# Keys and values of the dilated attention: projected in token order, then put into the group's order

## The chip, the cores and the metric

The kernel runs on one core of a Trainium2 chip. The metric is the device time of one execution in microseconds; the kernel before takes 1798.36 us (median of three runs, 1797.4 to 1800.12). One further execution was profiled, and every row below is from that one.

## What is computed

One transformer layer on 1024 tokens of width 1024, in float32. After a norm, the hidden states `h` are projected by one wide matrix. Its columns feed a gated linear attention and three groups of dilated attention (4 heads of 128). What matters here is a group's order of tokens:

```
DIL_PATTERNS = ((128, 1), (512, 4), (2048, 16))      # window, dilation
k = rms_norm(heads(k, 128), dil_k_norm_g[l, gi])     # q too; v without a norm
to_sub(t): t.reshape(B, S // dilation, dilation, H, E), the two token axes swapped, padded
           to blocks of 128: block b of residue d holds tokens d, d + dilation, ...
scores of a block of queries against its own and the previous block of keys, softmax, times v
```

Dilation 4 has four residues of 256 tokens, so two blocks each. Dilation 16 has sixteen of 64 tokens; the kernel puts two of them (d and d + 8) into one block of 128 and masks across them. Behind attention come the mix of the branches, the output projection, the router and the experts, which the change does not touch.

## The kernel before, in words

`h` is transposed and split into a high and a low part of fp32r (`hT`, tiles named strip, width first, tokens along the free dimension). Every weight quarter (128 x 1024, 512 KB) is loaded on SP's queue into `w_raw` (three buffers), and a cast on ScalarE (L131) and a subtraction on VectorE (L132) make its high and low part (`part`, five buffers). A matmul of the projections is three: high with high, high with low, low with high (`mm3`, L241 to L243).

A projection of one tile (`project`, L316) makes 128 tokens by 512 columns: eight steps over the width, three matmuls each, 24 in all. The stationary operand, which a weight load brings in before each matmul, is 128 tokens of `hT`; the moving one is 512 columns of weights. Which 128 tokens a tile holds is what `tokens` (L307) says: 128 neighbours for group 0 (dilation 1), every fourth of 512 for group 1 (dilation 4), every eighth of 1024 for group 2 (dilation 16). In the two wider groups the stationary operand is thus read with a step of four or eight elements, and the products come out in the group's order.

The groups go 2, 1, 0. `k_stage(g)` projects eight key tiles; `normed` (L336) squares a tile on ScalarE, sums on VectorE, takes the root on ScalarE, multiplies on VectorE, and one tile later four transposes on TensorE (L349, into one of two banks named tp) and a scaled copy on ScalarE (L350) put it into `kT` (tiles named ka, five buffers of two key tiles). `k_stage(2)` is woven into the last head's recurrence of the linear attention, four of its steps for one of the recurrence; `k_stage(1)` and `k_stage(0)` begin in the last three tiles of the attention before (L459) and finish alone.

`attention(g, ...)` projects eight value tiles, one after another without a transpose except the last key tile's behind value tile 0; each is copied out of its bank by ScalarE (L384) into tiles named kb. Then come queries 0, 1 and 2, each normalised and transposed like a key tile, scores (L403), softmax, transposes of the probabilities (L418) and the products with the values (L431), whose results go to DRAM (L435). The maxima and sums of the softmax go through DRAM into token order (L482 to L488) and are read back, much later in the program, by the combine stage (L687).

The program is written in one order. A scheduler then makes each engine's and each queue's order: it goes through time with its own costs, and an instruction whose inputs and buffers are ready is placed before one that is not, with program order deciding among those that are. Each engine and queue then works strictly in the order made. Dependencies on tiles, in DRAM too, become waits.

Of the kernel before, what the change touches and what calls it, by code (L numbers as in the profile page):

```python
# [9 lines left out]
F32 = mybir.dt.float32  # L10
# [5 lines left out]
AF = mybir.ActivationFunctionType  # L16
OP = mybir.AluOpType
# [3 lines left out]
S = 1024  # L21
# [3 lines left out]
NT = 8  # L25
# [119 lines left out]
def run(gen):  # L145

    while True:
        try:
            next(gen)
        except StopIteration as e:  # L150
            return e.value
# [20 lines left out]
def kernel_body(tc, out, x, w_in, w_alr, w_a2, gains, b_gate, w_mix, g1, g2, g2c, w_r, b_r, w_gate, w_up, w_down,  # L172
                c_mats, c_bias, c_slots):
    nc = tc.nc
    es = ExitStack()
    consts = es.enter_context(tc.tile_pool(name="consts", bufs=1))
    dram = es.enter_context(tc.tile_pool(name="dram", bufs=1, space=bass.MemoryType.DRAM))
# [12 lines left out]
    def acc():  # L190
        return ps_acc.tile([128, 512], F32, name="acc")

    def tp():
        return ps_tp.tile([128, 512], F32, name="tp")
# [6 lines left out]
    def t2k(shape=(128, 512), dt=F32):  # L201
        return work.tile(list(shape), dt, name="t2k", bufs=n2k)
# [4 lines left out]
    def ka4(shape=(128, 1024), dt=F32):  # L207
        return kv.tile(list(shape), dt, name="ka", bufs=5)

    def kb4(shape=(128, 1024), dt=F32):  # L210
        return kv.tile(list(shape), dt, name="kb", bufs=4)
# [3 lines left out]
    sr_dram = dram.tile([3, 64, 128], F32, name="sr_dram")  # L215
    st_dram = dram.tile([3, 8, S], F32, name="st_dram")
    f_dram = dram.tile([3, H, S], F32, name="f_dram")
    yg_dram = dram.tile([KT, 128, S], F32, name="yg_dram")
    zt_dram = dram.tile([NT, 128, KT, 128], F32, name="zt_dram")
    h2_dram = dram.tile([S, D], F32, name="h2_dram")  # L220
# [18 lines left out]
    def mm3(ps, a, b, first, last):  # L239
        (ah, al), (bh, bl) = a, b  # L240
        nc.tensor.matmul(ps, ah, bh, start=first, stop=False)  # L241
        nc.tensor.matmul(ps, ah, bl, start=False, stop=False)  # L242
        nc.tensor.matmul(ps, al, bh, start=False, stop=last)  # L243
# [14 lines left out]
    def rsqrt(rs, ss, n):  # L258
        nc.scalar.activation(rs, ss, AF.Ln, bias=eps, scale=1.0 / n)
        nc.scalar.activation(rs, rs, AF.Exp, scale=-0.5)  # L260
# [16 lines left out]
    for n in range(NT):  # L277
# [11 lines left out]
        for q in range(2):  # L289
            pt = tp()  # L290
# [9 lines left out]
    gcol = consts.tile([128, 7], F32, name="gcol")  # L300
# [6 lines left out]
    def tokens(ap, g, i):  # L307

        if g == 0:
            return ap[:, 128 * i:128 * i + 128]  # L310
        if g == 1:
            d, b = divmod(i, 2)
            return ap[:, 512 * b + d:512 * b + 512:4]
        return ap[:, i::8]

    def project(ps, g, i, units, act=None):  # L316

        act = act or hT
        for k in range(KT):
            hi, lo = units[k // 2]  # L320
            j = 512 * (k % 2)
            mm3(ps, (tokens(act[k][0], g, i), tokens(act[k][1], g, i)), (hi[:, j:j + 512], lo[:, j:j + 512]), k == 0, k == KT - 1)
            yield
# [12 lines left out]
    def normed(ps, gain, res):  # L336

        sq = t2k()
        nc.scalar.activation(sq, ps, AF.Square)  # L339
        ss = small.tile([128, 4], F32, name="ss4")  # L340
        nc.vector.tensor_reduce(ss, sq.rearrange("p (h e) -> p h e", h=4), axis=AX.X, op=OP.add)  # L341
        rs = small.tile([128, 4], F32, name="rs4")
        rsqrt(rs, ss, 128)
        nc.vector.tensor_tensor(sq.rearrange("p (h e) -> p h e", h=4), ps.rearrange("p (h e) -> p h e", h=4),
                                rs[:, :, None].to_broadcast([128, 4, 128]), op=OP.mult)
        yield
        pt = tp()
        for h in range(4):
            nc.tensor.transpose(pt[:, 128 * h:128 * h + 128], sq[:, 128 * h:128 * h + 128], ident)  # L349
        nc.scalar.activation(res, pt, AF.Copy, scale=gain)  # L350

    def k_stage(g):
        units = W.take(4)
        kT = []
        for i in range(NT):
            if i % 2 == 0:
                t = ka4()
            kT.append(t[:, 512 * (i % 2):512 * (i % 2) + 512])
        last = None
        for i in range(NT):  # L360
            ps = acc()
            yield from project(ps, g, i, units)
            if last is not None:
                run(last)
            last = normed(ps, gcol[:, 4 + g:5 + g], kT[i])
            next(last)
        return kT, last

    def attention(g, kT, last, after):
# [4 lines left out]
        units = W.take(4)  # L374
        v = []
        for i in range(NT):
            ps = acc()
            run(project(ps, g, i, units))
            if i == 0:
                run(last)  # L380
            if i % 2 == 0:
                t = kb4()
            v.append(t[:, 512 * (i % 2):512 * (i % 2) + 512])
            nc.scalar.copy(v[i], ps)  # L384
        units = W.take(4)

        def query(i):
            ps = acc()
            yield from project(ps, g, i, units)
            return ps  # L390
# [46 lines left out]
        def normq(ps):  # L437
            res = t2k()
            g_ = normed(ps, qg[:, g:g + 1], res)
            next(g_)  # L440
            return res, g_
# [12 lines left out]
        ps = run(query(2))  # L454
        run(qn[1][1])
        for i in range(NT):
# [12 lines left out]
            if i < NT - 3:  # L469
                ps = run(fill)  # L470
# [3 lines left out]
        pt = tp()  # L474
# [16 lines left out]
    units = W.take(4)  # L491
    v = []
    for b in range(NT):
        ps = acc()
        run(project(ps, 0, b, units))
        if b % 2 == 0:
            t = kb4()
# [14 lines left out]
    for hf in range(2):  # L512
        cols = slice(512 * hf, 512 * hf + 512)
        ps = acc()
# [48 lines left out]
    for j in range(2):  # L563
        t = kv.tile([128, 512], F32, name=f"att{j}", bufs=1)
# [78 lines left out]
    for h in range(H):  # L643
        _, qk = weave(recur(h, *qk), heads(h + 1) if h < H - 1 else k_stage(2), 2 if h < H - 1 else 4)

    units = {}

    def gr(j):

        if j % 2 == 0:  # L650
            units[j // 2] = W.take(1)[0]
        ps = acc()
        yield from columns(ps, cut(units[j // 2], 0, KT), j % 2)
        return ps
# [7 lines left out]
    for g in (2, 1, 0):  # L662
        after = k_stage(g - 1) if g > 0 else gr_start()
        attention(g, *qk, after)
        qk = run(after)
# [3 lines left out]
    for h in range(H):  # L669
        og = w4k()  # L670
        nc.sync.dma_start(og, og_dram[:, h])
        for hf in range(2):
            j = 2 * h + hf
            ps = qk[j] if j < 3 else run(gr(j))
            t = t2k()
# [28 lines left out]
    for c in range(KT):  # L704
# [3 lines left out]
        for hf in range(2):  # L708
            ps = acc()
# [79 lines left out]
    for e in range(NE):  # L789
        for w in (w_gate, w_up):  # L790
            v = w[e].rearrange("(p k) c -> p k c", k=KT)
            experts += [v[:, 2 * u:2 * u + 2] for u in range(4)]
        v = w_down[e].rearrange("(p k) c -> p k c", k=4)
# [304 lines left out]
    with tc.For_i(0, todo, 1) as i:  # L1098
        sp = (mybir.EngineType.SP,)
        e = nc.values_load(lst[0:1, bass.ds(i, 1)], engines=sp, min_val=0, max_val=NE - 1)  # L1100
        b = nc.values_load(lst[0:1, bass.ds(i + 16, 1)], engines=sp, min_val=0, max_val=6)
# [6 lines left out]
        v = w_down[bass.ds(e, 1)].rearrange("o (p k) c -> p (o k) c", k=4)  # L1108
# [26 lines left out]
```

## Time and profile before

| | |
|---|---|
| median of three runs | 1798.36 us |
| the profiled execution | 1798.59 us |
| its span (first to last instruction) | 1796.7 us |
| TensorE busy (matmuls) | 1763.9 us, 98% of the span |
| weight loads busy (beside matmuls) | 1493.9 us, 83% |
| VectorE, ScalarE, GpSimd busy | 59%, 50%, 6% |
| memory traffic | 324.44 MB, 181 GB/s in the mean |

PE is TensorE's matmuls, PEld its weight loads, which overlap the matmul before. A matmul's recorded duration is longer than its share of a stream, since matmuls are pipelined; the distance from start to start is what one costs. SPq is SP's queue, which issues nearly all transfers; its rows are issues and not transfers. Of the span, attention with its projections lies from about 200 to 760 us, the experts from about 1180 us on.

### The profile page before, as it was taken

The page shows a single profiled execution, that of the slowest core. Times are in us where ns is not written, and L with a number is a line of the kernel's source. Part 1 is how long each engine was busy: PE and PEld are TensorE (multiplying, and loading weights), DVE is VectorE, ACT ScalarE, POOL GpSimd, SP SyncE. Part 2 cuts the span into 40 slices and gives each one's busy share as a digit, 9 for nine tenths or more (in the row PEclk, how much of TensorE's full clock was granted, in tenths as well). Part 3 has the DMA queues.
Part 4 walks back from the last instruction along what each step waited for, and adds up shares of the span by engine and source line. Part 5 has one row for each costly group of instructions (what it writes and reads, how often), then busy time and mean ns, then how long its engine had stood idle before and what let it go on. Part 6 is the DMA issues. An engine that isn't in the chain of part 4 may idle for free.

```text
span 1796.7 us, 23091 instructions
## 1 busy us (share of the span) xinstructions
PE 1763.9 (98%) x8603; PEld 1493.9 (83%) x8603; DVE 1059.1 (59%) x1554; ACT 904.3 (50%) x1464; POOL 115.9 (6%) x110
## 2 busy tenths in 40 slices
PE   8999999999999999999999999999999999999996
PEld 7788899999998888887888878887777777777775
DVE  6375550442145225657232256769999899998985
ACT  6453341443244324433121143358787888888774
POOL 0000000000000000000000011121111111111110
PEclk9999999999999999999999999999999999999999
DMA  6111100122102110469331289579999999999992
GB/s 214 47 36 59 48 28 31 59 78 66 47 18 81 58 47 25 131 194 281 101 105 59 90 271 287 181 236 351 366 358 350 347 354 353 354 358 357 354 362 80
DMA packets 123217, 324.44 MB, mean 181 GB/s; under 512 B 25808, under 2 KB 42784, under 8 KB 123088
## 3 DMA queue, kind: packets, MB, share of 16 engines
q1 hardware_dynamic: 112512, 304.83, 48.2%
q0 software_dynamic: 10016, 17.78, 4.1%
q8 instruction: 68, 1.11, 0.3%
q10 hardware_dynamic: 576, 0.34, 0.1%
q14 instruction: 45, 0.37, 0.1%
HBM read 297.49 MB, written 42.43 MB: 189 GB/s over the span
## 4 chain that ended last, share of the span: by engine, by line
PE 75%; DMA 15%; DVE 5%; issue 2%; ACT 2%; SPq 0%; POOL 0%; DVEq 0%; POOLq 0%; ACTq 0%
PE acc L241 19%; PE acc L242 19%; PE acc L243 19%; DMA m_raw<-in_w_down_dram 3%; DMA m_raw<-in_w_up_dram 2%; DMA n_raw<-in_w_gate_dram 2%; DMA n_raw<-in_w_up_dram 2%; PE mm L241 2%; PE mm L243 2%; PE mm L242 2%; PE mm L403 2%; PE mm L431 2%; DVE part L132 1%; DVE m_part L132 1%; PE tp L349 1%
## 5 line engine op out<-in xcount | busy, mean ns | idle before, releaser
L132 DVE TENSOR_TENSOR part<-w_raw,part 128x1024 fp32r<-128x1024 f32 x111 | 135.5, 1221 | 256.3 <-ACT part L131 255.8
L241 PE MATMUL acc<-part,strip 128*128 128x512 f32 x640 | 276.0, 432 | 1.0 <-ACT part L131 1.0
L242 PE MATMUL acc<-part,strip 128*128 128x512 f32 x640 | 257.3, 402 | 1.5 <-DVE part L132 1.5
L243 PE MATMUL acc<-part,strip 128*128 128x512 f32 x640 | 256.6, 401 | 0.0
L132 DVE TENSOR_TENSOR part<-m_raw,part 128x1024 fp32r<-128x1024 f32 x173 | 209.4, 1221 | 26.7 <-ACT part L131 24.2
L131 ACT CAST part<-m_raw 128x1024 fp32r<-128x1024 f32 x173 | 180.5, 1055 | 45.6 <-PE acc L243 27.9
L241 PE MATMUL acc<-strip,part 128*128 128x512 f32 x448 | 181.7, 406 | 0.9 <-ACT t2k L747 0.9
L242 PEld LDWEIGHTS acc<-part,strip 128*128 128x128 f32 x640 | 172.6, 270 | 11.7 <-DVE part L132 2.3
L241 PEld LDWEIGHTS acc<-part,strip 128*128 128x128 f32 x640 | 170.3, 266 | 11.6 <-ACT part L131 1.7
L243 PEld LDWEIGHTS acc<-part,strip 128*128 128x128 f32 x640 | 170.6, 267 | 11.3 <-DVE strip L256 0.2
L243 PE MATMUL acc<-strip,part 128*128 128x512 f32 x448 | 176.2, 393 | 0.0
L242 PE MATMUL acc<-strip,part 128*128 128x512 f32 x448 | 175.5, 392 | 0.0
L131 ACT CAST part<-w_raw 128x1024 fp32r<-128x1024 f32 x111 | 116.6, 1051 | 108.7 <-PE acc L243 92.2
L132 DVE TENSOR_TENSOR m_part<-m_raw,m_part 128x1024 fp32r<-128x1024 f32 x104 | 126.5, 1218 | 5.4 <-ACT m_part L131 5.2
L241 PE MATMUL acc<-part,xT 128*128 128x512 f32 x320 | 128.1, 400 | 0.0
L243 PE MATMUL acc<-part,xT 128*128 128x512 f32 x320 | 126.8, 396 | 0.0
L242 PE MATMUL acc<-part,xT 128*128 128x512 f32 x320 | 125.9, 393 | 0.8 <-DVE part L132 0.8
L131 ACT CAST m_part<-m_raw 128x1024 fp32r<-128x1024 f32 x104 | 109.6, 1056 | 17.4 <-PE mm L243 8.7
L341 DVE TENSOR_REDUCE ss<-t2k 128x4 f32<-128x512 f32 x48 | 32.9, 685 | 133.6 <-ACT t2k L339 133.6
L241 PEld LDWEIGHTS acc<-strip,part 128*128 128x128 f32 x448 | 84.3, 188 | 18.9 <-ACT t2k L747 1.4
L243 PEld LDWEIGHTS acc<-strip,part 128*128 128x128 f32 x448 | 84.2, 188 | 18.7
L242 PEld LDWEIGHTS acc<-strip,part 128*128 128x128 f32 x448 | 84.3, 188 | 18.3 <-issue 1.2
(274 smaller groups left out, 3321.6 us busy)
## 6 DMA issues: line engine op xcount, KB each, us to landing
m_raw<-in_w_up_dram SPq DMA_DIRECT2D x96, 512.0 KB
m_raw<-in_w_gate_dram SPq DMA_DIRECT2D x91, 512.0 KB
m_raw<-in_w_down_dram SPq DMA_DIRECT2D x90, 512.0 KB
w_raw<-in_w_in_dram SPq DMA_DIRECT2D x52, 512.0 KB
w_raw<-in_w_mix_dram SPq DMA_DIRECT2D x32, 512.0 KB
n_raw<-in_w_down_dram SPq DMA_DIRECT2D x22, 512.0 KB
n_raw<-in_w_gate_dram SPq DMA_DIRECT2D x22, 512.0 KB
w4k<-in_x_dram SPq DMA_DIRECT2D x16, 512.0 KB
```

The source lines that it names most:

```text
L131: self.copies.append(self.nc.scalar.copy(hi, raw))
L132: self.last = self.nc.vector.tensor_tensor(lo, raw, hi.bitcast(F32), op=OP.subtract)
L241: nc.tensor.matmul(ps, ah, bh, start=first, stop=False)
L242: nc.tensor.matmul(ps, ah, bl, start=False, stop=False)
L243: nc.tensor.matmul(ps, al, bh, start=False, stop=last)
L341: nc.vector.tensor_reduce(ss, sq.rearrange("p (h e) -> p h e", h=4), axis=AX.X, op=OP.add)
L349: nc.tensor.transpose(pt[:, 128 * h:128 * h + 128], sq[:, 128 * h:128 * h + 128], ident)
L403: nc.tensor.matmul(ps[:, h2, 128 * c:128 * c + 128], qT[:, 128 * h:128 * h + 128], kT[j][:, 128 * h:128 * h + 128], start=True, stop=True)
L431: nc.tensor.matmul(po[:, 128 * h:128 * h + 128], v[j][:, 128 * h:128 * h + 128], pTs[c][:, 128 * h:128 * h + 128], start=c == 0, stop=c == ...
```

## The change

Keys and values of groups 1 and 2 are projected with the tokens in their own order (`project(ps, 0, i, units)`). Queries stay as they were.

Keys: the four transposes leave a tile of 128 tokens in a bank. Instead of one copy, four instructions spread it over the group's order, ScalarE and VectorE in turn: each takes 128 of the 512 columns with a step of four (group 1) or eight (group 2) elements and writes runs of 32 or 16. Tile n thus lands in all four pairs of key tiles.

Values: each tile is copied from its bank into a tile of the work pool and written to `v_dram`; when all eight are written, eight reads bring them back in the group's order, whole rows of 2 KB, every fourth or every eighth.

```diff
+    v_dram = dram.tile([2, S, 512], F32, name="v_dram")
...
-        nc.scalar.activation(res, pt, AF.Copy, scale=gain)
+        if callable(res):
+            res(pt)
+        else:
+            nc.scalar.activation(res, pt, AF.Copy, scale=gain)
...
+        def spread(n):
+
+            def res(pt):
+                for m in range(4):
+                    if g == 1:
+                        at = kT[2 * m + n // 4].rearrange("p (h t) -> p h t", h=4)[:, :, 32 * (n % 4):32 * (n % 4) + 32]
+                        src = pt.rearrange("p (h r d) -> p d h r", h=4, d=4)[:, m]
+                    else:
+                        at = pairs[m].rearrange("p (i h t) -> p i h t", i=2, h=4)[:, :, :, 16 * n:16 * n + 16]
+                        src = pt.rearrange("p (h r i) -> p i h r", h=4, i=8)[:, 2 * m:2 * m + 2]
+                    if m % 2 == 0:
+                        nc.scalar.activation(at, src, AF.Copy, scale=gain)
+                    else:
+                        nc.vector.tensor_scalar(at, src, gain, None, op0=OP.mult)
+            return res
...
-            yield from project(ps, g, i, units)
+            yield from project(ps, 0, i, units)
             if last is not None:
                 run(last)
-            last = normed(ps, gcol[:, 4 + g:5 + g], kT[i])
+            last = normed(ps, gain, spread(i) if g else kT[i])
...
-            run(project(ps, g, i, units))
+            run(project(ps, 0, i, units))
             if i == 0:
                 run(last)
...
+            if g:
+                t = t2k()
+                nc.scalar.copy(t, ps)
+                nc.sync.dma_start(v_dram[g - 1, 128 * i:128 * i + 128], t)
+            else:
...
+        if g:
+            for i in range(NT):
+                if i % 2 == 0:
+                    t = kb4()
+                v.append(t[:, 512 * (i % 2):512 * (i % 2) + 512])
+                d, b = divmod(i, 2)
+                nc.sync.dma_start(v[i], v_dram[0, 512 * b + d:512 * b + 512:4] if g == 1 else v_dram[1, i::8])
         units = W.take(4)
```

## Rows read from the trace of the kernel before

**Rows 1.** From the page: the span, and the share of the chain that ended last by engine.
```profile
span 1796.7 us, 23091 instructions
...
PE 75%; DMA 15%; DVE 5%; issue 2%; ACT 2%; SPq 0%; POOL 0%; DVEq 0%; POOLq 0%; ACTq 0%
```

**Rows 2.** Busy time of the engines in three stretches of nine projected tiles each (values 1 to 7, queries 0 and 1): groups 2, 1 and 0. Columns: stretch, its length, busy time of PE, PEld, DVE, ACT and POOL with the number of instructions, granted clock of TensorE, DMA share, GB/s.
```profile
274.36:327.46 53.10, 53.10 (x219) 53.03 (x218) 6.28 (x6) 10.44 (x16) 0.00 (x0) 1.00 0.12 40
443.34:495.01 51.67, 51.67 (x219) 51.60 (x218) 6.28 (x6) 10.44 (x16) 0.00 (x0) 1.00 0.13 45
616.25:666.74 50.49, 50.49 (x219) 40.65 (x218) 6.28 (x6) 10.44 (x16) 0.00 (x0) 1.00 0.14 48
```

**Rows 3.** Weight loads of the first of the three matmuls in the same three stretches, in that order: busy us, mean ns of one, idle us before them.
```profile
L241 PEld LDWEIGHTS acc<-part,strip 128*128 128x128 f32 x72 | 23.7, 329 | 0.0
...
L241 PEld LDWEIGHTS acc<-part,strip 128*128 128x128 f32 x72 | 22.3, 310 | 0.0
...
L241 PEld LDWEIGHTS acc<-part,strip 128*128 128x128 f32 x72 | 13.5, 188 | 3.2
```

**Rows 4.** TensorE's matmuls in order of time: start, duration. Group 2's first key matmul, the last of the woven key matmuls that stand behind other work and its successor, value tile 0 of group 2 and the transposes behind it; group 1's first key matmul and its successor, its value tile 0; value tile 0 of group 0.
```profile
202.72 0.80 PE L241 MATMUL acc<-part,strip 128*128 128x512 f32 x1
...
263.60 0.60 PE L241 MATMUL acc<-part,strip 128*128 128x512 f32 x1
264.04 0.42 PE L242 MATMUL acc<-part,strip 128*128 128x512 f32 x1
...
267.94 0.61 PE L241 MATMUL acc<-part,strip 128*128 128x512 f32 x1
...
274.01 0.60 PE L349 MATMUL tp<-mats,t2k 128*128 128x128 f32 x4
...
381.54 0.60 PE L241 MATMUL acc<-part,strip 128*128 128x512 f32 x1
381.97 0.40 PE L242 MATMUL acc<-part,strip 128*128 128x512 f32 x1
...
437.07 0.60 PE L241 MATMUL acc<-part,strip 128*128 128x512 f32 x1
...
442.98 0.60 PE L349 MATMUL tp<-mats,t2k 128*128 128x128 f32 x4
...
610.22 0.48 PE L241 MATMUL acc<-part,strip 128*128 128x512 f32 x1
610.53 0.40 PE L242 MATMUL acc<-part,strip 128*128 128x512 f32 x1
...
615.90 0.60 PE L349 MATMUL tp<-mats,t2k 128*128 128x128 f32 x4
```

**Rows 5.** Busy time as in rows 2, in three stretches of key tiles: tiles 3 to 7 of group 1, the same five of group 0, and group 2's eight tiles woven into the recurrence.
```profile
405.38:436.72 31.34, 31.34 (x143) 30.97 (x142) 9.78 (x14) 11.61 (x23) 2.28 (x8) 1.00 0.10 28
579.65:609.86 30.21, 30.21 (x142) 24.50 (x141) 9.73 (x14) 11.56 (x23) 2.25 (x8) 1.00 0.10 27
202.70:267.58 64.88, 64.88 (x340) 62.11 (x339) 31.25 (x60) 25.82 (x55) 0.00 (x0) 1.00 0.13 41
```

**Rows 6.** Groups of instructions by line and shape on ScalarE and VectorE, whole span: busy us, mean ns of one, idle us before them and who ended it. tp, acc and mm are PSUM banks; L1027 reads its bank with a step of four elements.
```profile
L350 ACT ACTIVATE ka<-tp,gcol 128x512 f32<-128x512 f32 x24 | 16.4, 685 | 1.2 <-PE tp L349 1.2
...
L599 ACT ACTIVATE t2k<-t2k 128x128 f32<-128x128 f32 x8 | 2.5, 312 | 3.2 <-DVE t2k L598 3.2
...
L1027 DVE TENSOR_TENSOR t2k<-t2k,acc 128x512 f32<-128x512 f32 x32 | 34.6, 1081 | 4.8 <-PE acc L243 4.5
L344 DVE TENSOR_TENSOR t2k<-acc,rs 128x512 f32<-128x512 f32 x48 | 33.1, 689 | 17.9 <-ACT rs L260 17.8
...
L622 DVE COPY state<-mm 128x128 f32<-128x128 f32 x4 | 1.2, 289 | 5.1 <-PE mm L616 5.1
```

**Rows 7.** TensorE in order of time: the transposes of query 0 of group 2, and its first products with values.
```profile
327.46 0.60 PE L349 MATMUL tp<-mats,t2k 128*128 128x128 f32 x4
...
339.82 1.05 PE L431 MATMUL mm<-t2k,kb 128*128 128x128 f32 x8
```

**Rows 8.** ScalarE in order of time, with the idle time before an instruction and what ended it: the copy of value tile 7 of group 2, the next cast of a weight quarter, and the cast after that one.
```profile
315.93 0.59 ACT L384 COPY kb<-acc 128x512 f32<-128x512 f32 x1 [0.41 <-PE acc L243]
317.07 1.05 ACT L131 CAST part<-w_raw 128x1024 fp32r<-128x1024 f32 x1 [0.56 <-DMA w_raw<-in_w_in_dram]
...
373.47 1.05 ACT L131 CAST part<-w_raw 128x1024 fp32r<-128x1024 f32 x1
```

**Rows 9.** Issues on SP's queue in order of time (neighbours of one line are merged): four weight quarters of group 1's keys, a first result of attention, two reads for the combine stage, the first weight quarter of the experts.
```profile
313.85 5.88 SPq L122 DMA_DIRECT2D w_raw<-in_w_in_dram  x4
...
341.63 0.33 SPq L435 DMA_DIRECT2D oa_dram<-t2k  x1
...
414.07 0.80 SPq L687 DMA_DIRECT2D sdc<-st_dram  x2
...
1051.45 0.33 SPq L122 DMA_DIRECT2D w_raw<-in_w_gate_dram  x1
```

**Rows 10.** Busy time as in rows 2, in the two half microseconds in which the packets of the result issued at 341.63 move; the last two columns are the DMA share and GB/s.
```profile
342.50:343.00 0.50, 0.50 (x5) 0.50 (x4) 0.00 (x0) 0.07 (x1) 0.00 (x0) 1.00 1.03 385
343.00:343.50 0.50, 0.50 (x3) 0.50 (x3) 0.00 (x0) 0.50 (x1) 0.00 (x0) 1.00 0.30 111
```

**Rows 11.** DMA packets of the stretch from 313 to 325 us, in which the four weight quarters of rows 9 move.
```profile
DMA packets 577, 2.11 MB, mean 175 GB/s; under 512 B 64, under 2 KB 64, under 8 KB 576
```

More of the change, by code (lines that the diff above doesn't have):

```diff
@@ L349, in normed @@
             nc.tensor.transpose(pt[:, 128 * h:128 * h + 128], sq[:, 128 * h:128 * h + 128], ident)
-        nc.scalar.activation(res, pt, AF.Copy, scale=gain)
+        if callable(res):
+            res(pt)
+        else:
+            nc.scalar.activation(res, pt, AF.Copy, scale=gain)
     def k_stage(g):
         units = W.take(4)
-        kT = []
+        kT, pairs = [], []
         for i in range(NT):
@@ L357, in k_stage @@
                 t = ka4()
+                pairs.append(t)
             kT.append(t[:, 512 * (i % 2):512 * (i % 2) + 512])
+        gain = gcol[:, 4 + g:5 + g]
+        def spread(n):
[12 more added lines that the diff above has]
+            return res
         last = None
@@ L377, in attention @@
             ps = acc()
-            run(project(ps, g, i, units))
+            run(project(ps, 0, i, units))
             if i == 0:
                 run(last)
[L381 to L384, printed above, removed]
+            if g:
[6 more added lines that the diff above has]
+                v.append(t[:, 512 * (i % 2):512 * (i % 2) + 512])
+                nc.scalar.copy(v[i], ps)
+        if g:
+            for i in range(NT):
+                if i % 2 == 0:
+                    t = kb4()
+                v.append(t[:, 512 * (i % 2):512 * (i % 2) + 512])
+                d, b = divmod(i, 2)
+                nc.sync.dma_start(v[i], v_dram[0, 512 * b + d:512 * b + 512:4] if g == 1 else v_dram[1, i::8])
         units = W.take(4)
```

## The prediction

> **What bounds the kernel now.** First the page. Of the chain that ended last TensorE holds 75% [rows 1]; so the question is what TensorE's own instructions cost in the stages that the change touches, and whether it ever waits there. Second, a table of stretches. Three stretches hold the same work, nine tiles of 24 matmuls without a transpose between them (values 1 to 7 and queries 0 and 1), for the dilations 16, 4 and 1: 53.10, 51.67 and 50.49 us [rows 2]. TensorE is busy for every microsecond of each at a granted clock of 1.00, so the difference is no wait. What differs is the column of weight loads: 53.03 and 51.60 us busy in the first two, 40.65 in the third. Third, the loads by shape: one takes 329 ns with tokens eight apart, 310 with tokens four apart, 188 with tokens side by side, and only the last leaves idle time between loads [rows 3]. The strided stationary operand is thus the limit of these stages, by a little: a tile costs 5.90, 5.74 and 5.61 us. Fourth, the order of TensorE's instructions. Behind other work the first load is not covered: first start to second start takes 0.44 us with stride eight (263.60), 0.43 with stride four (381.54), 0.31 with none (610.22) [rows 4].
>
> **What the change takes away.** For dilations 16 and 4, keys and values are projected with `tokens(..., 0, i)`; queries stay strided. The price per tile is then that of dilation 1, which the same lines show. The terms:
> - Values 1 to 7, dilation 16: 7/9 of 53.10 - 50.49 = 2.03 us. Dilation 4: 7/9 of 51.67 - 50.49 = 0.92 [rows 2].
> - Value tile 0, from its first matmul to the transposes behind it: 6.07, 5.91 and 5.68 us [rows 4], so 0.39 and 0.23.
> - Key tiles 3 to 7 of dilation 4 stand alone: 31.34 us against 30.21 for the same five of dilation 1 [rows 5], 1.13.
> - Key tiles 0 to 2 of dilation 4 are woven into the attention before: 72 matmuls, nine of them first ones behind other work (381.54 is the first of the nine). Nine times 0.43 - 0.31 is 1.08; the other 63 gain (1.18 - 0.12)/215 = 0.0049 us each, 0.31.
> - Key tiles of dilation 16 are woven into the last recurrence: 192 matmuls, 14 of them first ones (from 202.72 to 263.60 [rows 4]). 14 times 0.13 is 1.82; 178 times (2.61 - 0.13)/215 = 0.0115 is 2.05.
>
> Together 9.96 us. All of it is TensorE time on the chain. What comes later starts from TensorE's progress: the first expert weights are asked for at 1051.45 [rows 9], so the weight stream that fills the last 600 us moves forward with the rest.
>
> **What it adds.** *The spread of keys.* Per tile one ScalarE copy of 128x512 (685 ns) becomes two ScalarE and two VectorE instructions of 128x128. The trace has none of this shape from PSUM with a step. Nearest: ScalarE 128x128 in 312 ns, VectorE 128x128 from PSUM in 289 [rows 6]. A step is bounded by the VectorE product that reads PSUM with a step of four, 1081 against 689 ns without, 1.57 times. So ScalarE works 0.62 to 0.98 us per tile where it worked 0.69, and VectorE 0.58 to 0.91 more; in the densest stretch (eight tiles in 64.88 us) they are busy 25.8 and 31.3 us [rows 5], so eight tiles add at most 2.4 and 7.3 to engines that idle half of it. Side by side a spread lasts 0.6 to 1.0 us, one after another 1.2 to 1.9; tiles come six us apart and two banks take turns. I take nothing on the path: TensorE covers it. Without that cover it would cost up to 1.2 us a tile (1.9 - 0.7). A gain is excluded, since TensorE waits for nothing in these stretches [rows 5]. The scores need all eight key tiles now, but the last one's transposes are at 274.01 [rows 4] and no score comes ahead of query 0's at 327.46 [rows 7].
> [...] No row here has ScalarE and VectorE in one bank at once.
> *The values through DRAM.* The copy out of PSUM stays, with another target. Eight writes and eight reads of 256 KB per dilation are new on SP's queue. Dilation 16: the last copy ends at 316.52 [rows 8]; a write of this size was issued at 341.63 and its packets end by 343.5 [rows 9, 10], 1.9 us. The reads are 2.1 MB: 5.4 us at 385 GB/s [rows 10], 12 us at the 175 GB/s that four weight loads made [rows 11]. The first value tile would be in by about 321, the last by 331, with the weight loads in the way by 343. The first user is at 339.82 [rows 7], and each later tile's user comes later still. So nothing on the path; the cover is about 19 us for tile 0. Dilation 4 has the same order of stages.
> *What the reads hold up.* SP's queue goes in order and the reads wait for the last write. Behind them in program order come the weight loads for the next keys, now at 313.85 [rows 9]. The first of these is wanted at 317.07 by a cast on ScalarE [rows 8], and behind that cast stands query 0's normalisation, which TensorE's transposes at 327.46 need [rows 7]. The order on a queue is the scheduler's, which takes what is ready: a load of the combine stage, traced after all attention, is already issued at 414.07 [rows 9]. I take it that the weight loads, ready first, go first, and put nothing down; the other value is the second rival. The remaining three casts come from 373.47 on and have 50 us.
>
> Sum: the profiled execution took 1798.59 us (span 1796.7 [rows 1], 1.9 around it); 1798.59 - 9.96 = 1788.6. The median of the runs is 0.23 lower, so **1788.5**. Its own range is 1785.5 to 1790.5: the runs lie 1 to 2 us about their median, and the counts of first matmuls may shift by a few.
>
> **Rivals.** (1) *The spread shows.* One after another, with ScalarE held by VectorE's queue, a spread that reached TensorE in each of the eight woven tiles costs 8 x 1.2 = 9.6 us: 1798 if all of it shows, 1793 to 1794 if half. For it: the recurrence's own steps wait for the same two engines. Against it: TensorE waits for neither in 64.88 us [rows 5]. It decides from the point where a tile's spread and normalisation no longer fit in six us.
> (2) *The reads block the weights: slower.* If the reads stand first, they are issued at about 319 to 322, and the weight load behind them lands after their 5.4 to 12 us, at 331 to 337, not 317. ScalarE's cast stands in order, so query 0's normalisation starts 9.5 us late or more; 0 to 6 us of that are slack (query 0 ends one tile, 5.9 us, ahead of 327.46). That is 3.5 to 16 us per dilation. It decides from 5 us per dilation, where it eats the gain; at a middling 9 us it gives 1788.5 + 18 = 1806.5. For it: the trace order. Against it: the load at 414.07.
> (3) *Only the steady step falls.* If the 0.12 us of the first matmuls has another cause than the stride, 2.9 us in the woven stretches and 0.8 in the others stay: 1792.2. Against it: 0.31 at 610.22 is the same line behind the same transposes.
> That nothing falls, because the loads are not what bounds these stages, is nearly excluded by [rows 2, 3]: same lines, same matmuls, other stride.
>
> **How the numbers follow.** Forecast 0.80, first rival 0.06 (half of it above 1794.8), second 0.08, third 0.06. This kernel's measurement tells 0.2% (3.6 us) from no change, so faster means below 1794.8 and slower above 1802.0. Faster: 0.80 + 0.06 + 0.03 = 0.89; same 0.03 from the first rival and 0.01 from the second's low end; slower 0.07. The range runs from the low end of the forecast's, 1785.5, over the third rival to 1793.5, half of the first: 0.89 of the chance, and allowance for terms that are read from one execution.
>
> **What would show it.** Right: weight loads of 188 ns in the key and value stages of all dilations, the strided ones left only in the queries; value tiles of 5.6 us; 0.31 us at the first matmuls; TensorE's wait column empty; the first expert load ten us earlier. Spreads of 0.3 to 0.5 us each, and value reads that land over ten us ahead of their first user. Wrong: a gap in TensorE ahead of query 0's transposes with ScalarE's cast waiting for a weight load (second rival); waits for ScalarE or VectorE between 200 and 270 us (first); or value tiles that still take 5.9 us.

## The result, and the profile after

The changed kernel takes 1788.75 us, the median of 7 runs (1786.88 to 1793.97). The kernel before, run on the same chip, takes 1797.72 (1796.14 to 1801.33). The ratio is 0.9948, with a 95% interval of 0.9939 to 0.9958: faster by 0.5%, 9 us. The forecast was 1788.5 us. A second comparison on another chip gave 0.9944 (0.9924 to 0.9963).

First the page of the profiled execution: its span, the busy time of the engines, the shares of the chain that ended last.

```profile
span 1786.8 us, 23212 instructions
...
PE 1756.8 (98%) x8603; PEld 1452.1 (81%) x8603; DVE 1066.8 (60%) x1586; ACT 904.7 (51%) x1480; POOL 116.3 (7%) x110
...
PE 79%; DMA 13%; DVE 4%; issue 2%; ACT 2%; SPq 0%; POOL 0%; POOLq 0%; DVEq 0%; ACTq 0%
```

The span is 9.9 us shorter than in [rows 1]. TensorE's share of the chain has grown, from 75% to 79%, and that of DMA has fallen from 15% to 13%. These are shares of the whole span; whether TensorE waits in the touched stages is read below.

Next the touched stretch as a whole, from the first key matmul of group 2 to the transposes of group 1's sums. First the kernel before, then the changed one (start and end; length; busy time and instructions of PE, PEld, DVE, ACT, POOL; granted clock; DMA share; GB/s).

```profile
202.72:579.54 376.82, 376.82 (x1881) 365.88 (x1880) 136.55 (x221) 138.49 (x344) 2.28 (x8) 1.00 0.16 53
```

```profile
203.72:570.64 366.92, 366.92 (x1881) 321.87 (x1880) 145.06 (x253) 138.37 (x360) 2.32 (x8) 1.00 0.23 77
```

The same 1881 matmuls take 9.90 us less. TensorE is busy for all of both stretches; the weight loads fall by 44 us, VectorE works 8.5 us more, ScalarE as much as before, and the queues carry 45% more bytes per second. That is the whole gain: outside the stretch the changed execution came 1.0 us late to its start (in the first 20 us its granted clock was 0.83, where the kernel before had 1.00, in stages that the change does not touch), and was 0.9 us shorter again behind all attention (from 745 us on). The profiled execution of a second comparison (*changed_again*, below) has 366.91 us in the same stretch.

Now the stages. The same table for the three runs of nine projected tiles, which answer to [rows 2], and for group 2's woven and group 1's stand-alone key tiles, [rows 5]. Here a stretch begins with its first matmul or with the transposes ahead of it, and ends with transposes.

```profile
271.36:322.37 51.01, 51.01 (x219) 43.38 (x218) 6.98 (x8) 10.49 (x17) 0.00 (x0) 1.00 0.33 111
435.38:486.09 50.71, 50.71 (x219) 43.07 (x217) 6.98 (x8) 10.49 (x17) 0.00 (x0) 1.00 0.38 128
607.35:657.84 50.49, 50.49 (x220) 40.65 (x219) 6.28 (x6) 10.44 (x16) 0.00 (x0) 1.00 0.14 47
203.72:264.95 61.23, 61.23 (x340) 49.82 (x339) 34.19 (x72) 26.09 (x61) 0.00 (x0) 1.00 0.12 42
398.77:428.98 30.21, 30.21 (x143) 24.53 (x142) 12.31 (x24) 11.20 (x28) 2.32 (x8) 1.00 0.10 26
```

53.10 has become 51.01, 51.67 has become 50.71, and 31.34 has become 30.21, which is group 0's own figure. What is left over 50.49 in the first two is the two query tiles, still strided. The loads show it. First values 1 to 7 of group 2, then the query tiles of the same run (busy us, mean ns of one, idle us before them); [rows 3] had 329 ns for all nine.

```profile
L242 PEld LDWEIGHTS acc<-part,strip 128*128 128x128 f32 x56 | 10.5, 188 | 2.5
...
L244 PEld LDWEIGHTS acc<-part,strip 128*128 128x128 f32 x15 | 4.9, 329 | 0.0
```

TensorE in order of time, for [rows 4 and 7]: the last of the woven key matmuls that stand behind other work and its successor, the transposes around value tile 0, those of query 0, and the first product with values.

```profile
261.21 0.48 PE L242 MATMUL acc<-part,strip 128*128 128x512 f32 x1
261.53 0.39 PE L243 MATMUL acc<-part,strip 128*128 128x512 f32 x1
...
264.95 0.60 PE L350 MATMUL tp<-mats,t2k 128*128 128x128 f32 x4
...
271.00 0.60 PE L350 MATMUL tp<-mats,t2k 128*128 128x128 f32 x4
...
322.37 0.60 PE L350 MATMUL tp<-mats,t2k 128*128 128x128 f32 x4
...
334.78 0.49 PE L466 MATMUL mm<-t2k,kb 128*128 128x128 f32 x3
```

Start to start at the first matmul is now 0.32 us, where stride eight had 0.44. Query 0's transposes come 5.1 us earlier than in [rows 7].

The spread by line, over the whole span (the pieces of ScalarE and those of VectorE, with the idle time before them and what ended it), for [rows 6]:

```profile
L377 ACT ACTIVATE ka<-tp,gcol 128x128 f32<-128x128 f32 x32 | 11.6, 362 | 2.7 <-DVE ka L379 1.7 <-PE tp L350 1.0
L379 DVE TENSOR_SCALAR ka<-tp,gcol 128x128 f32<-128x128 f32 x32 | 11.0, 345 | 9.6 <-ACT ka L377 9.6
```

A piece lasts 362 or 345 ns, which is 1.16 and 1.19 times the 312 and 289 ns of the nearest rows, not 1.57. (The 1.57 was not the price of a step in the read: as L1027 is written, its last index runs over neighbours in the bank, and it is the result that is written 128 columns apart. ScalarE's nearest row does not read PSUM, so for ScalarE the step and the bank are not told apart.) The releasers are the other thing to see: VectorE waits 9.6 us for ScalarE's pieces and ScalarE 1.7 for VectorE's. The four pieces of a bank go one after another: in all sixteen spreads a piece starts after the one before it has ended, 0.03 us later at the least. What keeps them apart is not shown. From the start of its first piece to the end of its last, a spread lasts 1.5 to 2.4 us, and one of the sixteen 3.8. TensorE waits for none of it: in 195 to 600 us its list of waits is empty.

Last SP's queue in order of time around group 2's values, for [rows 9] (start, time from first to last of the merged issues, count).

```profile
308.98 1.74 SPq L122 DMA_DIRECT2D w_raw<-in_w_in_dram  x2
311.46 0.33 SPq L407 DMA_DIRECT2D v_dram<-t2k  x1
311.88 3.06 SPq L122 DMA_DIRECT2D w_raw<-in_w_in_dram  x2
316.45 3.86 SPq L419 DMA_DIRECT2D kb<-v_dram  x8
```

The four weight loads went ahead of the eight reads, as was taken. The reads' packets end at about 325 (371 GB/s in 323 to 324 us, 14 in 325 to 326), ten us ahead of the first product with values at 334.78. The first expert weights are asked for at 1042.77, 8.7 us earlier than in [rows 9], or 9.7 counted from the first key matmul.

### The profile page after: what moved, and what is told of

It reads as the page before. It is cut to its first block, busy times and chain, and to the rows that moved or that the text cites. A ratio compares the mean times of both kernels' runs of the same rounds, so it can differ in the third digit from the quotient of the medians.

```text
span 1786.8 us, 23212 instructions
## 1 busy us (share of the span) xinstructions
PE 1756.8 (98%) x8603; PEld 1452.1 (81%) x8603; DVE 1066.8 (60%) x1586; ACT 904.7 (51%) x1480; POOL 116.3 (7%) x110
## 4 chain that ended last, share of the span: by engine, by line
PE 79%; DMA 13%; DVE 4%; issue 2%; ACT 2%; SPq 0%; POOL 0%; POOLq 0%; DVEq 0%; ACTq 0%
PE acc L242 20%; PE acc L243 20%; PE acc L244 20%; DMA m_raw<-in_w_down_dram 3%; PE mm L242 2%; PE mm L244 2%; PE mm L243 2%; DMA n_raw<-in_w_gate_dram 2%; PE mm L438 2%; PE mm L466 2%; DMA m_raw<-in_w_up_dram 2%; DMA m_raw<-in_w_gate_dram 2%; DVE part L132 1%; PE tp L350 1%; PE mm L639 1%
## 5 line engine op out<-in xcount | busy, mean ns | idle before, releaser
L242 PE MATMUL acc<-part,strip 128*128 128x512 f32 x640 | 270.2, 422 | 1.0 <-ACT part L131 1.0
L243 PE MATMUL acc<-part,strip 128*128 128x512 f32 x640 | 256.4, 401 | 0.7 <-DVE part L132 0.7
L244 PE MATMUL acc<-part,strip 128*128 128x512 f32 x640 | 255.3, 399 | 0.0
L244 PEld LDWEIGHTS acc<-part,strip 128*128 128x128 f32 x640 | 137.8, 215 | 23.0 <-DVE strip L257 0.2
L243 PEld LDWEIGHTS acc<-part,strip 128*128 128x128 f32 x640 | 138.6, 217 | 21.5 <-DVE part L132 1.8
L242 PEld LDWEIGHTS acc<-part,strip 128*128 128x128 f32 x640 | 137.4, 215 | 21.6 <-ACT part L131 1.2
```

## The experiments

The theory is the prediction's: a strided stationary operand makes a weight load so long that it sets TensorE's pace, the change takes that away for two of three projections, and what it adds is hidden. The rivals: the spread shows, the reads hold up the weights, only the steady step falls. The first matmuls above (0.32 us) already speak against the third. "The touched stretch" is the one shown above, 376.82 and 366.92 us.

**One part alone.** *keys_only* is the changed kernel with values as before:

```diff
-            run(project(ps, 0, i, units))          # values
-            if g: ... v_dram write, eight reads
+            run(project(ps, g, i, units))
+            nc.scalar.copy(v[i], ps)
```

> The changed kernel with the values as before (strided projection, no DRAM). If the gain is the price of the strided weight loads and nothing that was added shows (the theory of the prediction), the key terms alone remain: 3.87 + 1.13 + 1.39 = 6.4 us below the kernel before, a ratio of 0.9964. If the spread shows in the woven tiles (first rival) and the values carry more of the gain than reckoned, it is 3 us or less, 0.9983 or nearer to 1.

Measured: 1794.85 us, ratio 0.9972 (0.9962 to 0.9982), touched stretch 370.79 us, 6.03 less. *values_only* is the reverse, keys as before with their single copy:

> The kernel before with only the values projected in token order and sent through DRAM. Theory: the value terms alone, 2.03 + 0.92 + 0.39 + 0.23 = 3.6 us below the kernel before, 0.9980. If the reads hold up the weights (second rival) it is slower than before. If keys and values together gain by something that neither has alone (another order of the queues), the two ratios don't add up to that of the changed kernel, 0.9948.

Measured: 1795.56 us, 0.9983 (0.9972 to 0.9995), touched stretch 373.25, 3.57 less. The two add up to 9.60 of the 9.90: no part pays for the other. The missing 0.3 is in keys_only, in the stage of group 2's strided values: from value tile 0's transposes to query 0's it takes 53.71 us, where the kernel before takes 53.45 (274.01 to 327.46), with weight loads of 331 to 332 ns instead of 327 to 332 and 0.247 us from matmul to matmul instead of 0.245. Attention itself gains the same 1.5 us in both. Why the same strided tiles took 0.26 us more is not shown.

**Does what was added cost anything?** *bare* has the token order without the spread and without DRAM:

```diff
-            yield from project(ps, g, i, units)    # keys
+            yield from project(ps, 0, i, units)
-            run(project(ps, g, i, units))          # values
+            run(project(ps, 0, i, units))
```

> The kernel before with keys and values of the wider groups projected in token order and left there: no spread, no trip through DRAM, so attention of these groups works on the wrong order of tokens. It has the whole gain and none of the added work. Theory: the added work is hidden, so it takes what the changed kernel takes, 0.9945 to 0.9950 of the kernel before. If the added work shows anywhere, it is faster than the changed kernel by what shows, 1 us (0.9940) or more.

Measured: 1790.41 us, 0.9953 (0.9938 to 0.9968), touched stretch 366.88. The changed kernel has 366.92: spread and DRAM together cost 0.04 us of TensorE's time. *spread_one_engine* puts more work on ScalarE, with all four pieces there and none on VectorE (`if m % 2 == 0:` becomes `if True:`):

> The changed kernel with all four pieces of a key tile's spread on ScalarE (4 x 0.36 = 1.45 us) and none on VectorE. The spreads of both engines wait for each other in the trace of the changed kernel. Theory: both forms are hidden behind six us of matmuls a tile, so the time is the same within 1 us. If ScalarE's order is near the path in the woven tiles (first rival), each of the eight loses up to 0.7 us: 5 us slower.

Measured: 1789.13 us, 0.9948 (0.9929 to 0.9966), touched stretch 366.89. ScalarE's 64 pieces take 18.4 us of its time in that stretch, where its 32 took 11.6, and nothing of it shows:

```profile
L377 ACT ACTIVATE ka<-tp,gcol 128x128 f32<-128x128 f32 x64 | 18.4, 372 | 1.0 <-PE tp L350 1.0
```

But a single spread became shorter by it, not longer: four pieces in a row on ScalarE take 1.1 to 1.7 us (the 18.4 us are 1.15 for each of the sixteen), where the alternation of two engines took 1.5 to 2.4. So this run tests a busier ScalarE and not a slower spread. What ends the first rival is *bare*, together with the empty list of waits. *twice* sends the values through DRAM two times:

```diff
+            nc.sync.dma_start(v2_dram[g - 1], v_dram[g - 1])
-                nc.sync.dma_start(v[i], v_dram[...])
+                nc.sync.dma_start(v[i], v2_dram[...])
```

> The changed kernel with the values going through DRAM twice: written, copied to a second place in DRAM by one transfer of 2 MB, read from there. It makes the trip longer by a transfer's 2 us and 2 MB read and written, some 8 to 15 us in all. In the trace of the changed kernel the reads end at 324.5 and the first product with values starts at 334.8. Theory: cover of 10 us and more, so less than 1 us is lost: 1788 to 1790. If the trip is nearer to the path than it looks, TensorE waits ahead of the first products, up to 5 us per dilation: 1799.

Measured: 1789.64 us, 0.9957 (0.994 to 0.9975), touched stretch 366.88. SP's queue in group 2:

```profile
315.40 0.58 SPq L415 DMA_DIRECT2D v_dram<-v_dram  x1
324.36 3.67 SPq L421 DMA_DIRECT2D kb<-v_dram  x8
```

The reads are issued 7.9 us later than in the changed kernel and no product waits: of the cover of ten us 7.9 are shown to be there.

**The second rival.** *reads_first* forces the order that the rival needs on SP's queue, the reads ahead of the weight loads:

```diff
+            with tc.issue_after(back.ins):         # back: the last read
+                units = W.take(4)
```

> The changed kernel with the loads of the next weights put behind the value reads on SP's queue (an ordering edge, no change in work): the order that the second rival feared. By that rival query 0's normalisation then stands behind a cast that waits for its weights and TensorE waits 3.5 to 16 us per dilation: 1796 to 1820 us. If the cast is put behind the normalisation as well, or the slack covers it, nothing changes: 1788 to 1790.

Measured: 1789.09 us, 0.9945 (0.9929 to 0.9962), touched stretch 367.41, 0.5 more. But the rival had two links, and in group 2 only the first was made: ScalarE's own order had moved with it. The cast that answers to the one at 317.07 in [rows 8], at 312.28 and ahead of query 0's square in the changed kernel, stood behind that square, at 323.62, and held up nothing. In group 1 the scheduler left the cast ahead of query 1's square. There it waited 3.4 us for its weights, until 485.09, query 0's scaled copy stood behind it, and TensorE waited for that copy:

```profile
PE mm L441 <- ACT t2k L354: 0.3, 1, 0.3
```

From query 0's transposes to query 1's it took 7.83 us there instead of 7.31, which is the 0.5. So the rival's mechanism showed, at a small price. *reads_then_cast* makes the second link in both groups, query 0's square behind the cast of the first of these loads:

```diff
+            ps = run(query(0))
+            with tc.issue_after(W.copies[-4].ins): # the cast
+                qn = {0: normq(ps)}
```

> The changed kernel with the second rival's whole chain made by hand, in both wide groups: the eight value reads ahead of the weight loads on SP's queue, and on ScalarE the cast of the first of these loads ahead of query 0's square. The rival as predicted: query 0's normalisation starts after the cast, 3.5 to 16 us are lost per dilation, 1795 to 1815 us. The other theory: the load is issued at about 316.7 as in the kernel with the reads first, lands behind the reads at 323 to 325, the cast ends at 324 to 326 and query 0's transposes can start at 327 to 329 where they stood at 322.4; but with that order TensorE's own order puts them behind query 2's projection, at 328.3, so that the touched stretch grows from 366.9 us by 0 to 4 us in all, 1789 to 1793 us.

Measured: 1791.86 us, 0.996 (0.9946 to 0.9974), touched stretch 368.30 (202.88 to 571.18), 1.4 more than in the changed kernel. ScalarE and then TensorE in order of time (idle before and what ended it in brackets):

```profile
323.69 1.05 ACT L131 CAST part<-w_raw 128x1024 fp32r<-128x1024 f32 x1 [13.09 <-DMA w_raw<-in_w_in_dram]
324.64 1.08 ACT L340 ACTIVATE t2k<-acc 128x512 f32<-128x512 f32 x2
...
327.94 0.66 PE L350 MATMUL tp<-mats,t2k 128*128 128x128 f32 x4 [0.38 <-DVE t2k L345]
```

Here is the rival's mechanism in full: ScalarE sits 13.1 us before the cast, waiting for the weight load, and query 0's square starts at 324.64 instead of 316.72. Yet TensorE waits 0.38 us. Its order had been laid out anew around the late square: query 2's projection now stands ahead of query 0's transposes and fills the time. The rest of the 1.4 us is no wait; in the new order eight more matmuls of the projections stand behind other work. The mechanism was real; the price of 3.5 to 16 us per dilation was not, because it left the order of TensorE as it was. (The scheduler knew of both ordering edges when it made that order; what a late load costs that it does not foresee is shown only by the 0.3 us above.)

**What the loads cost, and where the limit lies.** *strides* is the kernel before with other steps between the columns of the stationary operand: 2 and 3 in the keys and values of group 2, 6 and 7 in those of group 1; queries keep 8 and 4.

```diff
+        if g >= 10:
+            return ap[:, 0:128 * (g - 10):g - 10]
```

> As bare, but the stationary tokens are read with other steps: keys of group 2 every 2nd element, values of group 2 every 3rd, keys of group 1 every 6th, values of group 1 every 7th (always from token 0 on, so the wrong tokens). One look at the weight loads by stage; queries keep 8 and 4. [...] If any step costs the full price, step 2 shows 310 too. If the price grows evenly with the step, 2 costs about 205 to 230 and 6 and 7 lie between 310 and 329.

Measured, one execution: 1790.28 us. The loads of steps 2, 3, 6, 7, 8 and 4, in that order (stretches 205 to 260, 275 to 309, 405 to 426, 442 to 475, 322 to 380, 490 to 540 us):

```profile
L241 PEld LDWEIGHTS acc<-part,strip 128*128 128x128 f32 x58 | 11.3, 195 | 1.8
...
L241 PEld LDWEIGHTS acc<-part,strip 128*128 128x128 f32 x49 | 12.3, 251 | 0.0
...
L241 PEld LDWEIGHTS acc<-part,strip 128*128 128x128 f32 x27 | 8.2, 304 | 0.0
...
L241 PEld LDWEIGHTS acc<-part,strip 128*128 128x128 f32 x47 | 14.9, 316 | 0.0
...
L243 PEld LDWEIGHTS acc<-part,strip 128*128 128x128 f32 x53 | 17.4, 329 | 0.1
...
L243 PEld LDWEIGHTS acc<-part,strip 128*128 128x128 f32 x42 | 13.0, 310 | 0.0
```

And what a step from matmul to matmul takes, by the starts: with step 3, seven in 1.63 us; with step 7, six in 1.42.

```profile
275.21 0.40 PE L241 MATMUL acc<-part,strip 128*128 128x512 f32 x1
...
276.84 0.39 PE L242 MATMUL acc<-part,strip 128*128 128x512 f32 x1
```

```profile
447.77 0.40 PE L241 MATMUL acc<-part,strip 128*128 128x512 f32 x1
...
449.19 0.40 PE L241 MATMUL acc<-part,strip 128*128 128x512 f32 x1
```

That is 0.233 us with step 3, as with step 1, and 0.237 with step 7; 0.238 with steps 4 and 6, 0.245 with step 8. So the loads have no idle time left from step 3 on, but TensorE loses nothing at 251 ns, 4 to 5 ns per matmul at 304 to 316, and 11 at 329. In this run the loss came only with a full column of weight loads, but step 3 has such a column too and no loss.

**The queries too.** *queries_bare* is the changed kernel with the queries projected in token order as well (`project(ps, g, i, units)` in `query` becomes `project(ps, 0, i, units)`):

> The changed kernel with the queries of the wider groups projected in token order too and not put into the group's order afterwards, so the queries of these groups are the wrong ones. What is left of the price: for group 2 two tiles of 0.29 us and six woven ones with 24 first matmuls at 0.13 and 120 at 0.0115, 5.1 us; for group 1 two tiles of 0.13 and six with 21 first at 0.12 and 123 at 0.0049, 3.4 us. Theory: 8.5 us below the changed kernel, 1780.3. If the woven stages are set by scores and softmax and not by TensorE, less than 4 us.

Measured: 1781.11 us, 0.9898 (0.9881 to 0.9914), touched stretch 359.44, 7.48 less than in the changed kernel. To use this, the queries have to be put into the group's order: *queries_too* normalises the queries in token order, sends them through DRAM like the values, and weaves the next group's value tiles into the attention, where the strided queries stood; the next group's queries and keys then stand alone. The diff is shown in outline:

```diff
+    def q_stage(g, last=None): ... project(ps, 0, i, units), normed, write to q_dram
+        def read(i): ... t <- in_order(q_dram[g - 1], g, i)
+        def turn(t): four transposes, one ScalarE copy with the gain
-        qn = {0: normq(run(query(0)))} ...
+            qr = {0: read(0), 1: read(1)} ...
```

It was run with 12 of the buffers that hold the tiles on their way (the kernel before has nine) and, as *queries_too_9*, with nine, beside the changed kernel once more, *changed_again*.

> A version that goes on from the changed kernel: the queries of the wider groups are projected and normalised in token order, go through DRAM and come back a tile at a time in the group's order; the values of the next group, in token order, are now the work woven into attention; 12 buffers t2k in place of 9. No projection reads its tokens with a step. If what is added stays hidden, it takes what the run with unordered queries took, 8 us less than the changed kernel: 1780 to 1782. If the trips through DRAM reach the path (the queries' reads share the queue with weights, and the first value tile has about 10 us of cover), 1 to 8 us of it are lost.

> The same with 9 buffers t2k as in the changed kernel. The read-back tiles of the queries take buffers that the softmax needs. If buffers are short, TensorE waits and 2 us or more are lost against the run with 12; if not, the two agree within 1 us.

> The changed kernel once more, on the chip of the two runs beside it, to compare them directly: 1788 to 1790, 0.995 of the kernel before.

Measured: 1786.26 us with 12 (0.9928, 0.9903 to 0.9954), 1783.83 with nine (0.9908, 0.9889 to 0.9928), 1789.67 for the changed kernel (0.9944, 0.9924 to 0.9963). So queries_too_9 is the fastest whole version, by 0.9% against the kernel before and by some 0.3% against the changed one (their intervals, both against the kernel before, just overlap); it missed what was expected of it. From the first key matmul to the end of all attention (the transposes of group 0's sums at 738.96 us) it takes 536.2 us, where the changed kernel takes 541.4 and queries_bare 534.0. Of the 2.2 us between, 1.3 are a wait that the values never had, three times for a query from DRAM, at the start of attention:

```profile
PE tp L447 <- DMA t2k<-q_dram: 1.3, 3, 0.5
```

The 12 buffers cut that wait to 0.6 us and the stretch to 535.9, and yet their time was longer: behind attention their profiled execution took 1046.6 us where nine took 1042.8, in stages with the same work. In the other profiled executions here these stages took 1040.0 to 1045.0 us, whatever the kernel, so most of what the medians differ by may come from there. The intervals of the two overlap, and why 12 were not faster was not followed.

## Why the prediction was right

**The bound.** That the step of the stationary operand sets the pace in stages where TensorE is never idle is shown by *bare* and *values_only*: same matmuls, other stride, and 366.88 and 373.25 us where the kernel before took 376.82. The loads go with it, 329 and 310 ns with the step and 188 without; by what way they hold up the matmuls is not shown. One sign that the prediction read, no idle time left between loads, was weaker than it looked: with step 3 there was none either, and TensorE lost nothing (0.233 us from start to start). The comparison of stages with the same matmuls carried the forecast.

**The terms.** Measured between the same transposes in both traces:

| term | forecast, us | measured, us |
|---|---|---|
| keys of dilation 16, woven | 3.87 | 3.63 |
| value tile 0, dilation 16 | 0.39 | 0.38 |
| values 1 to 7, dilation 16 | 2.03 | 2.08 |
| key tiles 0 to 2 of dilation 4, woven | 1.39 | 1.52 |
| key tiles 3 to 7 of dilation 4 | 1.13 | 1.13 |
| value tile 0, dilation 4 | 0.23 | 0.22 |
| values 1 to 7, dilation 4 | 0.92 | 0.96 |
| attention of dilation 4 | 0 | -0.02 |
| sum | 9.96 | 9.90 |

The stand-alone tiles come out to a few hundredths, because their price was read from a stage that already had the new form. The woven ones were put together from a count and two prices and miss by 0.24 and 0.13, in opposite directions. For dilation 16 one of the fourteen first matmuls, that at 202.72, gained nothing: 0.64 us to the next start in both kernels. The other thirteen gained 0.127 us in the mean where 0.13 was taken. For dilation 4 the count was wrong: not nine but eleven first matmuls went from 0.43 or 0.44 us to 0.32, since two more key matmuls behind other work, at 380.38 and 381.07, stand ahead of the one at 381.54. That the sum came within 0.06 us is in part the luck of these opposite errors. That the median came within 0.3 us of 1788.5 is luck too: the runs lie between 1786.88 and 1793.97, and the terms as summed give 1788.4.

**What was costed at nothing.** The spread: the pieces went one after another, at 1.5 to 2.4 us and once 3.8, where the prediction had 1.2 to 1.9 for that case; the turns between the engines and their other work between pieces had been left out of its sum. Hidden all the same, by *bare*. The values through DRAM: hidden, by *bare* and *twice*. The cover for the first value tile was put at about 19 us, with arrival by 321; the reads were issued at 316.45 behind the weight loads and ended near 325, and the first product had itself moved forward to 334.78, so ten us were left. The order on SP's queue was as taken. Group 1's reads did not wait for all eight writes, since each needs only four of the tiles: they went in two lots, four at 455.13 and four at 480.32.

**The rivals.** The first fell: TensorE waited for no spread, though most lasted longer than the prediction's upper bound. The third fell at the first matmuls. The second did not arise, and was mis-sized: built in full it costs 1.4 us for both dilations, not 7 to 32. What failed in it was that TensorE would stand still while ScalarE waits.

**A miss in the experiments.** For queries_bare 8.5 us was expected and 7.48 came. Of the 1.0 us between, 0.4 is in the attentions' first matmuls: 22 in each group gained 0.124 and 0.115 us, where 24 and 21 of them at 0.13 and 0.12 had been counted; the rest was not traced. queries_too was expected at 1780 to 1782 and came to 1783.8 at best. Of the latter 1.3 us is the wait shown; the rest was not traced.

## What to carry to other kernels

Where TensorE shows no idle time, compare stages that hold the same matmuls, and look at the weight loads: a strided stationary operand cost 4 to 11 ns per matmul here with steps of four to eight, and a stage with the other layout gave the price of the stand-alone tiles to within 0.05 us. A full column of loads alone was not yet a loss (251 ns each with step 3, and 0.233 us from matmul to matmul as without a step). Reordering after the matmul, on engines that idle and through DRAM, cost 0.04 us here because the users came later, the values' ten us and the keys' fifty; where the user came at once, as for the first queries, 1.3 us of it showed. Splitting one bank between two engines did not shorten its reading: one engine alone was done in 1.1 to 1.7 us, two in 1.5 to 2.4. Before pricing a blocked queue, ask whether TensorE has other ready work that can be put in front: here it took in nearly all of a 13.1 us wait and left 0.38.

## What the runs showed of the hardware

A weight load of 128 fp32 columns took 188 ns with columns side by side, 195 two apart, 251 three apart, 304 to 310 four and six apart, 316 seven and 329 eight apart. Two apart thus costs next to nothing (7 ns), three apart lies between, four and six apart cost the same, and seven and eight apart cost 6 and 19 ns more than four. Neither of the two forms expected of it came: a price that any step pays in full would have given 310 two apart, one that grows evenly 205 to 230. No run here settles why. That a load of 251 ns fits into a step of 233 ns was not expected either: with step 3 the view from 275 to 309 us holds 49, 49 and 48 loads of the three lines, which add up to 36.7 us (12.3, 12.3 and 12.1) in a window of 34, so their records overlap. The 251 ns of such a record are therefore not the time for which a load keeps the next one off. That the stride is what slows the matmuls is shown (0.233 us from start to start side by side, 0.238 with steps of four, 0.245 of eight); by what way a long load delays the next matmul is not.
